# Broadcasting a norm's factor with eight narrow products instead of a diagonal, and another order of the second MLP pair's products

## The chip, the core and the metric

The kernel runs on one core of one Trainium2 chip. The core has a matrix engine (TensorE, PE in the profile; its weight loads are shown apart as PEld), a vector engine (VectorE, DVE), a scalar engine (ScalarE, ACT), a general engine (GpSimd, POOL) and a queue that issues DMA transfers (SyncE, SP). The metric is the device time of one execution in microseconds (us), lower is better.

## What is computed

One decoder layer over 1024 positions of width 1024, in float32. Cut to what matters here:

```python
h = rmsnorm(x, mix_norm)
q, k, v, su, sv, g_a, g_b = split(h @ w_in)
y_att = sliding_window_attention(q, k, v, q_norm, k_norm, sinks)
y_sgu = chunked_spatial_gating(su, sv, sgu_norm, w_s, b_s)
x = x + (sigmoid(g_a) * (y_att @ w_oa) + sigmoid(g_b) * (y_sgu @ w_ob)) @ w_out
z = rmsnorm(x, ffn_norm) @ w_up              # 1024 x 5632
z = conv_b + sum(conv_w[t] * shift(z, t) for t in range(3))   # causal, over positions
gate, val = split(z)                         # 2816 columns each
x = x + (silu(gate) * val) @ w_down
```

`rmsnorm(x, g)` is `x * rsqrt(mean(x * x) + 1e-6) * g`, with one factor per position.

## The kernel before, in words

The activations lie transposed: features on the 128 partitions, the 1024 positions along the row. A factor per position must therefore stand on every partition as a row of 1024 numbers, the tile `rstd_b`. It is first found as a column: position s * 128 + p on partition p, in column s of a 128 x 8 tile.

Every matrix product is made from numbers split into a high and a low part (`h` and `l`, type fp32r): high by high, high by low, low by high. ScalarE copies the high part (line 75), VectorE or GpSimd subtracts it to get the low one (line 974 for the weights of the MLP, on GpSimd).

**The broadcast.** `rms_rows` (line 120) turns the column into the row. VectorE makes a diagonal `diag` from the identity and the column (128 x 8 x 128); TensorE multiplies a matrix of ones with it, 512 columns at a time (line 123); ScalarE copies the result to `rstd_b` (line 125). These products are plain float32. It is done twice:
- In the prologue, for the first norm: the diagonal is made at line 322, the two halves are multiplied at lines 390 and 393, among the products of the queries (`q_proj`, lines 79 to 81) and the transposes of the keys (`k_trans`, line 338).
- In the MLP, for the second norm: `ssq_cols` (line 1338) multiplies the sums of squares with ones to get the column, VectorE and GpSimd turn it into the factor (GpSimd the power, line 116), and the diagonal is made at line 1349. Here the factor is a ratio: the activations were scaled before with the first norm's factor.

**The pairs.** The MLP's first half takes the 44 blocks of 128 columns of `w_up` in 22 pairs, a gate block and a value block. Each pair is computed with 7 products instead of 8, by sums and differences of the blocks (the scheme of Strassen and Winograd). A product is `prod(out, left, right)`: 12 matmuls, 4 steps of the contraction with three parts each, into one PSUM half of 512 columns. Left operands are weights: A11 and A12 (tile `p`, parts `ph` and `pl`), S1 and A22 (tile `q`, parts `qh` and `ql`), S3 (tile `s3`), S2 and S4 (the sums `lr` by GpSimd at line 608, parts in the tile AX). Right operands (B11, B21, B22, T1 to T4) are the activations, kept for all pairs. `more=True` adds onto what the output holds.

A pair has a gate accumulator (`g0`, `g1`) and a value accumulator (`v0`, `v1`). Copies of partial results in SBUF (`x1`, `x7`, `u2`) are added by VectorE in `sums` and `last_sum`; `scale` multiplies by `rstd_b`. Then come the convolution (`tap_v` and `tap_g` on ScalarE, line 1362, `conv` on VectorE, line 1367), `tanh` on ScalarE and `gated` on VectorE (lines 1390 and 1391), and the results go to memory. All that belongs to the previous pair runs while the current pair is multiplied.

**The order.** From the MLP on, and in the prologue's part around line 390, the order is written out by hand: every engine takes its instructions in the order of the program text. `first_pair` (line 1432) multiplies pair 0 and prepares pair 1: `nx.split_p`, `nx.split_s3`, `ssq_cols`, `nx.sums_r` (two `lr` on GpSimd), `nx.split_q` (`qh` on ScalarE, `ql` on GpSimd), `nx.split_r` (AX). Its results can't be scaled yet, as the factor isn't there. So the second pair (pair 1) is multiplied by `fast_pair` with `rms` given: the closure `rms` (line 1481) broadcasts the ratio into the PSUM tile of the second pair's own value accumulator, scales the first pair and adds its last sum. All later pairs call `fast_pair` with `rms=None`. The weight tiles are double buffered: `qh` and `ql` of a pair reuse the space that S1 and A22 of the pair before read; the tile of `s3h` is single.

The second pair's products before: A11, (broadcast), A12, S3, S1, A22, S2, S4.

Of the kernel before, what the change touches and what calls it, by code (L numbers as in the profile page):

```python
# [10 lines left out]
F = mybir.dt.float32  # L11
# [3 lines left out]
ALU = mybir.AluOpType  # L15
# [26 lines left out]
def body(ctx, tc, nc, a):  # L42
    L, H = slice(0, 512), slice(512, 1024)
# [6 lines left out]
    def nm(s):  # L50
        uid[0] += 1
        return f"{s}_{uid[0]}"
# [8 lines left out]
    def PS(s):  # L61
        pools_ = psum["P"]
        pools_.append(pools_.pop(0))
        return pools_[-1].tile([128, 1024], F, tag="P", name=nm(s))

    def PH(s):
        if psum.get("H") is None:
            return PS(s)[:, 0:512]
        return psum["H"].tile([128, 512], F, tag="H", name=nm(s))
# [32 lines left out]
    ident = base.tile([128, 128], F, name="ident")  # L102
    ones = base.tile([128, 128], F, name="ones")
    mh05 = base.tile([128, 16], F, name="mh05")
    rstd_b = base.tile([128, 1024], F, name="rstd_b")
    rstd = base.tile([128, 8], F, name="rstd")
# [6 lines left out]
    def rsqrt_cols(dst, ss, n, width):  # L113

        nc.vector.tensor_scalar(dst, ss, 1.0 / width, EPS, op0=ALU.mult, op1=ALU.add)
        return nc.gpsimd.tensor_tensor(dst, dst, mh05[:, :n], op=ALU.pow)

    msk = base.tile([128, 4, 128], U8, name="msk")

    def rms_rows(pb, diag, hs=(0, 1)):  # L120

        for h, p in zip(hs, pb):
            nc.tensor.matmul(p, ones, diag[:, h * 4:(h + 1) * 4, :], start=True, stop=True)
        for h, p in zip(hs, pb):
            nc.scalar.copy(rstd_b[:, h * 512:(h + 1) * 512], p)  # L125

# [48 lines left out]
    pa = pa_cm.__enter__()  # L175
# [30 lines left out]
    for k in range(8):  # L206
# [8 lines left out]
        for s in range(8):  # L215
            o = pkv[s // 4][:, (s % 4) * 256:(s % 4 + 1) * 256]
            c = slice(s * 128, (s + 1) * 128)
# [35 lines left out]
    def q_sq(n):  # L253
        p = st.pop(("pq", n)).rearrange("p (h d) -> p h d", d=64)
        sq = qp.tile([128, 4, 64], F, tag="qsq", name=nm("qsq"), bufs=2)
        nc.scalar.activation(sq, p, AF.Square)
        st[("q", n)] = [p, sq]
# [20 lines left out]
    def q_split(n):  # L278
        p = st.pop(("qT", n))
        qs = qp.tile([128, 2, 256], R, tag="qs", name=nm("qs"), bufs=2)  # L280
        for g in range(2):
            copy_hi(qs[ROWS[g], g, :], p[ROWS[g], :])
        for g in range(2):
            nc.vector.tensor_tensor(qs[ROWS[1 - g], g, :], p[ROWS[g], :], qs[ROWS[g], g, :].bitcast(F),
                                    op=ALU.subtract)
        st[("qT", n)] = qs
# [13 lines left out]
    for s in range(8):  # L300
        nc.tensor.matmul(p_ssq[:, 2 * s:2 * s + 2], sqsum[:, s * 128:(s + 1) * 128], ones[:, 0:2],
                         start=True, stop=True)
# [9 lines left out]
    for h in range(2):  # L312
# [5 lines left out]
    nc.vector.tensor_tensor(kss3, kss3, rstd2.unsqueeze(2).to_broadcast([128, 8, 2]), op=ALU.mult)  # L318
    rsqrt_cols(krs[:, 0:8], kss[:, 0:8], 8, 64)
    rsqrt_cols(krs[:, 8:16], kss[:, 8:16], 8, 64)  # L320
    diag = pa.tile([128, 8, 128], F, tag="sq", name="diag")
    nc.vector.tensor_tensor(diag, ident.unsqueeze(1).to_broadcast([128, 8, 128]),
                            rstd.unsqueeze(2).to_broadcast([128, 8, 128]), op=ALU.mult)
    q_sq(0)
    q_sq(1)

# [60 lines left out]
    q_split(0)  # L387
    q_trans(1)
    q_split(1)
    rms_rows([PH("rb")], diag, (0,))  # L390
    q_proj(3)
    k_trans(1)
    rms_rows([PH("rb")], diag, (1,))
    q_sq(2)
    v_split()
    q_ms(2)
# [320 lines left out]
    rb = sg.tile([128, 512], F, name="rb")  # L717
# [620 lines left out]
    def ssq_cols(p):  # L1338
        for s in range(8):
            nc.tensor.matmul(p[:, 2 * s:2 * s + 2], pools["sq2"][:, s * 128:(s + 1) * 128], ones[:, 0:2],  # L1340
                             start=True, stop=True)
        pool = pools["fp"]
        ss = pool.tile([128, 8], F, name="ss8b")
        nc.vector.tensor_copy(ss, p[:, 0:16].rearrange("p (s two) -> p s two", two=2)[:, :, 0])
        rsqrt_cols(ss, ss, 8, D)
        nc.vector.reciprocal(rstd, rstd)
        nc.vector.tensor_tensor(ss, ss, rstd, op=ALU.mult)
        diag = pool.tile([128, 8, 128], F, tag="ac", name="diag2", bufs=2)
        nc.vector.tensor_tensor(diag, ident.unsqueeze(1).to_broadcast([128, 8, 128]),
                                ss.unsqueeze(2).to_broadcast([128, 8, 128]), op=ALU.mult)  # L1350
        return diag

    class Pair(Blocks):

# [77 lines left out]
    def first_pair():  # L1432
        w, nx = lefts[0], lefts[1]
        z = PS("pz"), PS("pz")
        q, q2 = Pair(0, w.w, z[::-1]), Pair(1, nx.w)
        xu = pools["fp"].tile([128, 1024], F, tag="h", name="xu", bufs=2)
        x7, u2 = xu[:, L], xu[:, H]
        x1 = pools["fp"].tile([128, 512], F, tag="ac", name="x1", bufs=2)

        def late_split(n, r, eng):  # L1440
            comb[n] = Y(n, R, [128, 2, 4, 512])
            for k in range(0, 4, 2):
                src, h = pools[r][:, k:k + 2, :], comb[n][:, 0, k:k + 2, :]
                copy_hi(h, src)
                eng.tensor_tensor(comb[n][:, 1, k:k + 2, :], src, h.bitcast(F), op=ALU.subtract)

        q.prod(q.v1, "A11", "B11")
        nc.scalar.copy(x1, q.v1)
        w.split_r(0)
        nx.load_p()  # L1450
        q.prod(q.g0, "A12", "B21")
        late_split("T2", "raw2", nc.vector)
        nx.load_q()
        nx.load_s3()
        q.prod(q.g1, "S1", "T1")
        nc.scalar.copy(u2, q.g1)
        late_split("T4", "raw4", nc.gpsimd)
        for c, p in zip((L, H), late["px"]):
            nc.scalar.activation(p, late["ac"][:, c], AF.Square)
            nc.vector.tensor_tensor(pools["sq2"][:, c], pools["sq2"][:, c], p, op=ALU.add)  # L1460
        q.prod(q.v0, "S3", "T3")
        nc.scalar.copy(x7, q.v0)
        nx.split_p()
        nx.split_s3()
        nc.vector.tensor_tensor(x7, x7, u2, op=ALU.add)
        q.prod(q.g1, "S4", "B22", more=True)
        nc.vector.tensor_tensor(q.g0, q.g0, x1, op=ALU.add)
        q.prod(q.v1, "S2", "T2", more=True)
        pb = q2.zv
        diag = ssq_cols(pb)  # L1470
        nx.sums_r()
        nx.split_q()
        lefts[2].load_p()
        q.prod(q.v0, "A22", "T4", more=True)
        nc.scalar.copy(u2, q.v1)
        q.u2 = u2
        nx.split_r(1)
        nc.vector.tensor_tensor(q.v1, u2, x7, op=ALU.add)
        nc.vector.tensor_tensor(q.v0, u2, q.v0, op=ALU.add)

        def rms():

            rms_rows([pb[:, L], pb[:, H]], diag)
            q.scale(q.zv)
            q.last_sum()

        pools["ft_cm"] = tc.tile_pool(name="ft", bufs=1, reuse_waits="tile")
        return q, q2, rms

    def fast_pair(n, prev, q, hooks, rms=None):  # L1490

        nx = lefts[n + 1] if n + 1 < NPAIR else None

        def temp(t, p="ft"):
            return pools[p].tile([128, 512], F, tag=t, name=nm(t), bufs=2 if p == "ft" else 1)

        if rms:
            x1 = temp("x1f", "wx")
        else:
            prev.last_sum()  # L1500
            prev.tap_v()
            x1, x7, q.u2 = temp("x1"), temp("x7"), temp("u2")
        q.prod(q.g0, "A11", "B11")
        if nx:
            nx.load_q()
            nx.load_s3()
        else:
            hooks[2]()
        nc.scalar.copy(x1, q.g0)  # L1509
        if rms:  # L1510
            rms()
            pools["fp_cm"].__exit__(None, None, None)
            pools["ft"] = pools["ft_cm"].__enter__()
            x7, q.u2 = temp("x7"), temp("u2")
            prev.tap_v()
            q.prod(q.g0, "A12", "B21", more=True)
        prev.tap_g()
        prev.conv()
        q.prod(q.v0, "S3", "T3")
        if nx:  # L1520
            nx.split_s3()
        nc.scalar.copy(x7, q.v0)
        if not rms:
            q.prod(q.g0, "A12", "B21", more=True)
        if rms:
            nx.split_p()
        prev.tanh()
        if not rms:
            prev.gated()
        q.prod(q.g1, "S1", "T1")  # L1530
        if nx and not rms:
            nx.split_p()
        nc.vector.tensor_tensor(x7, x7, q.g1, op=ALU.add)
        if rms:
            prev.gated()
        prev.stores()
        if nx:
            nx.sums_r()
        if n + 2 < NPAIR:
            lefts[n + 2].load_p()  # L1540
        q.prod(q.v0, "A22", "T4", more=True)
        if nx:
            nx.split_q()
            nx.split_r(n + 1)
        else:
            hooks[0]()
        q.prod(q.v1, "S2", "T2")
        q.sums(x1, x7, q.v0)
        if not nx:
            hooks[1]()  # L1550
        q.prod(q.g1, "S4", "B22", more=True)
        return q

    SUM_AT = (2, 4, 5, 7, 8, 10)
# [280 lines left out]
```

## Time and profile before

| | us |
|---|---|
| median of 3 runs | 1198.6 |
| lowest and highest | 1198.53, 1199.31 |
| profiled execution, first to last instruction (span) | 1196.2 |
| TensorE busy in the span | 1183.4 (99%) |
| VectorE busy | 881.4 (74%) |
| ScalarE busy | 543.0 (45%) |
| GpSimd busy | 574.4 (48%) |
| matmuls of the MLP's pairs and the gates (line 1014), share of the chain that ended last | 42% |

For the profiled execution the span is all the time that is known; the median of the runs lies 2.4 us above it, which is what lies around the span.

A row of the timeline has the start and the duration in us, the engine, the line, the operation, output <- inputs, the shape, and how often it came in a row (xN); in brackets stands how long the engine was idle before it, and what ended that. A matmul shows a duration longer than the distance to the next one, since matmuls are pipelined: the pace is read from the starts. A row of waits has the engine and line that waited, what it waited for, the total in us, how often, and the longest. Names are those of tiles, with the buffer numbers left out.

### The profile page before, as it was taken

What the parts mean: (1) busy time and instruction counts of PE and PEld (TensorE: products, weight loads), DVE (VectorE), ACT (ScalarE), POOL (GpSimd) and SP (SyncE); (2) the same over time, 40 slices, a digit from 0 to 9 for tenths busy, and PEclk for the clock granted to TensorE, in tenths of its full rate; (3) what the DMA queues carried; (4) which work ended last, traced back from release to release, by engine and by line L of the source; (5) the groups of instructions that cost most, each with busy time, mean ns of one, the idle gap of its engine ahead of it and who ended that gap; (6) DMA issues with size and microseconds to landing.
All of it is one profiled execution on the core that took longest, in us unless ns stands there. A gap on an engine that the chain in (4) does not pass through costs nothing.

```text
span 1196.2 us, 15840 instructions
## 1 busy us (share of the span) xinstructions
PE 1183.4 (99%) x5866; PEld 1002.4 (84%) x5866; DVE 881.4 (74%) x1028; ACT 543.0 (45%) x832; POOL 574.4 (48%) x365
## 2 busy tenths in 40 slices
PE   9999999999999999999999999999999999999998
PEld 9889989988888888888788888888888888888886
DVE  8788975755638565668887788878788788775674
ACT  8555567644335222234444444444444445434331
POOL 2467685588668222344866575656657541000000
PEclk9999999999999999999999999999999999999999
DMA  7010143037786997342143342423333268975471
GB/s 283 23 53 19 54 139 126 11 122 271 237 308 206 358 320 273 128 166 98 45 150 108 104 136 102 149 89 123 109 129 124 87 205 290 370 235 194 150 238 61
DMA packets 79133, 191.27 MB, mean 160 GB/s; under 512 B 8912, under 2 KB 9168, under 8 KB 79056
## 3 DMA queue, kind: packets, MB, share of 16 engines
q1 hardware_dynamic: 79056, 190.26, 46.2%
q8 instruction: 46, 0.75, 0.3%
q14 instruction: 31, 0.25, 0.1%
HBM read 139.63 MB, written 50.59 MB: 159 GB/s over the span
## 4 chain that ended last, share of the span: by engine, by line
PE 82%; DVE 7%; ACT 4%; POOL 3%; DMA 2%; issue 2%; SPq 0%; ACTq 0%; POOLq 0%; DVEq 0%
PE pz L1014 42%; PE pd L1661 10%; PE pdy L1661 8%; PE po L80 2%; PE po L79 2%; PE po L81 2%; PE px L79 2%; PE px L80 2%; PE px L81 2%; DMA ls<-wup 1%; PE pvs L81 1%; PE pvs L79 1%; PE pvs L80 1%; ACT x L75 1%; PE pq L79 1%
## 5 line engine op out<-in xcount | busy, mean ns | idle before, releaser
L1014 PE MATMUL pz<-T,qh 128*128 128x512 f32 x472 | 145.6, 390 | 0.0
L1014 PE MATMUL pz<-B,ph 128*128 128x512 f32 x352 | 108.5, 389 | 0.7 <-ACT x1f L1509 0.7
L974 POOL TENSOR_TENSOR pl<-lp,ph 128x1024 fp32r<-128x1024 f32 x30 | 72.5, 2418 | 75.4 <-ACT ph L75 75.3
L1014 PEld LDWEIGHTS pz<-T,qh 128*128 128x128 f32 x472 | 88.4, 188 | 18.6 <-ACT u L865 0.3
L1014 PE MATMUL pz<-T,ql 128*128 128x512 f32 x236 | 91.8, 389 | 0.0
L96 POOL TENSOR_TENSOR wjl<-wj,wjh 128x512 fp32r<-128x512 f32 (+1 forms) x24 | 40.6, 1693 | 95.7 <-ACT wjh L75 95.7
L974 POOL TENSOR_TENSOR ql<-lq,qh 128x1024 fp32r<-128x1024 f32 x30 | 77.9, 2597 | 9.1 <-ACT qh L75 9.1
L1014 PEld LDWEIGHTS pz<-B,ph 128*128 128x128 f32 x352 | 66.0, 188 | 15.2 <-ACT x1f L1509 1.5
L1030 DVE TENSOR_TENSOR pz<-pz,rstd_b 128x1024 f32<-128x1024 f32 x60 | 73.9, 1232 | 3.3 <-ACT rstd_b L125 1.3
L974 POOL TENSOR_TENSOR s3l<-s,s3h 128x512 fp32r<-128x512 f32 x29 | 38.5, 1328 | 73.4 <-ACT s3h L75 73.4
L1014 PE MATMUL pz<-T,s3h 128*128 128x512 f32 x232 | 71.7, 390 | 0.0
L1014 PE MATMUL pz<-B,pl 128*128 128x512 f32 x176 | 68.5, 389 | 0.0
L1661 PE MATMUL pd<-bl,ah 128*128 128x512 f32 x176 | 68.5, 389 | 0.0
L1661 PE MATMUL pd<-bh,al 128*128 128x512 f32 x176 | 68.5, 389 | 0.0
L1661 PE MATMUL pd<-bh,ah 128*128 128x512 f32 x176 | 68.5, 389 | 0.0
L75 ACT ACTIVATE qh<-lq 128x1024 fp32r<-128x1024 f32 x30 | 31.8, 1061 | 72.0 <-POOL pl L974 36.6
L1014 PE MATMUL pz<-T,AX 128*128 128x512 f32 x264 | 63.4, 389 | 0.0
L1014 PE MATMUL pz<-B,AX 128*128 128x512 f32 x264 | 63.4, 389 | 0.0
L1014 PEld LDWEIGHTS pz<-T,AX 128*128 128x128 f32 x264 | 49.5, 188 | 10.3
L1014 PEld LDWEIGHTS pz<-B,AX 128*128 128x128 f32 x264 | 49.5, 188 | 10.3
L1367 DVE SCALAR_TENSOR_TENSOR tg<-pz,cp,tg 128x1023 f32<-128x1023 f32 (+1 forms) x44 | 56.2, 1278 | 0.8
L1367 DVE SCALAR_TENSOR_TENSOR tv<-pz,cp,tv 128x1023 f32<-128x1023 f32 (+1 forms) x44 | 56.2, 1277 | 0.8
(343 smaller groups left out, 3549.6 us busy)
## 6 DMA issues: line engine op xcount, KB each, us to landing
ls<-wup SPq DMA_DIRECT2D x22, 512.0 KB, 5.7
sum<-ls SPq DMA_DIRECT2D x22, 512.0 KB, 5.1
lp<-wup SPq DMA_DIRECT2D x22, 512.0 KB, 3.5
ra<-wdown SPq DMA_DIRECT2D x44, 256.0 KB, 4.8
b<-T SPq DMA_DIRECT2D x44, 256.0 KB, 3.8
B<-tv SPq DMA_DIRECT2D x33, 256.0 KB, 2.0
T<-tt SPq DMA_DIRECT2D x33, 256.0 KB, 2.1
b<-B SPq DMA_DIRECT2D x33, 256.0 KB, 3.5
```

The source lines that it names most:

```text
L75: return nc.scalar.activation(dst, src, AF.Copy, scale=scale)
L79: nc.tensor.matmul(out, wh, mh, start=first, stop=False, **kw)
L80: nc.tensor.matmul(out, wh, ml, start=False, stop=False, **kw)
L81: nc.tensor.matmul(out, wl, mh, start=False, stop=last, **kw)
L96: nc.gpsimd.tensor_tensor(l[:, :nk, :], r[:, :nk, :], h[:, :nk, :].bitcast(F), op=ALU.subtract)
L974: nc.gpsimd.tensor_tensor(l, r, h.bitcast(F), op=ALU.subtract)
L1014: nc.tensor.matmul(o, p[:, k, :], y[:, q, k, :], start=not more and k == 0 and j == 0, stop=k == 3 and j == 2, skip_group_check=True)
L1030: nc.vector.tensor_tensor(z, z, rstd_b, op=ALU.mult)
L1367: nc.vector.scalar_tensor_tensor(t[:, j:], p[:, 0:1024 - j], cw[:, ci, 2 - j:3 - j], t[:, j:], op0=ALU.mult, op1=ALU.add)
L1661: nc.tensor.matmul(o[d], p[:, k - k0, m], q[:, k - k0, :], start=new and k == 0 and j == 0, stop=k == HK - 1 and j == 2, skip_group_check= ...
```

## The change

The broadcast takes the column itself as weights: for each of the 8 columns, a product with 128 times the same column as stationary operand (a repeat with a step of zero) and the identity as moving operand gives 128 entries of the row, on all partitions. Four such products fill what one product of 512 columns filled before. Both diagonals are gone.

In the second pair, S1 goes ahead of the broadcast, S4 behind A12, and S2 ahead of A22. So the order is A11, S1, (broadcast), A12, S4, S3, S2, A22. The copy `x7` is taken from S1's result instead of S3's, and S3's result is added to it. The other pairs keep their order.

```diff
-    def rms_rows(pb, diag, hs=(0, 1)):
+    def rms_rows(pb, col, hs=(0, 1)):
         for h, p in zip(hs, pb):
-            nc.tensor.matmul(p, ones, diag[:, h * 4:(h + 1) * 4, :], start=True, stop=True)
+            for s in range(4):
+                c = 4 * h + s
+                nc.tensor.matmul(p[:, s * 128:(s + 1) * 128], col[:, c:c + 1].to_broadcast([128, 128]), ident,
+                                 start=True, stop=True)
...
-    diag = pa.tile([128, 8, 128], F, tag="sq", name="diag")
-    nc.vector.tensor_tensor(diag, ident.unsqueeze(1).to_broadcast([128, 8, 128]),
-                            rstd.unsqueeze(2).to_broadcast([128, 8, 128]), op=ALU.mult)
...
-    rms_rows([PH("rb")], diag, (0,))
+    rms_rows([PH("rb")], rstd, (0,))
...
-    rms_rows([PH("rb")], diag, (1,))
+    rms_rows([PH("rb")], rstd, (1,))
...
         nc.vector.tensor_tensor(ss, ss, rstd, op=ALU.mult)
-        diag = pool.tile([128, 8, 128], F, tag="ac", name="diag2", bufs=2)
-        nc.vector.tensor_tensor(diag, ident.unsqueeze(1).to_broadcast([128, 8, 128]),
-                                ss.unsqueeze(2).to_broadcast([128, 8, 128]), op=ALU.mult)
-        return diag
+        return ss
...
         nc.scalar.copy(x1, q.g0)
         if rms:
+            q.prod(q.g1, "S1", "T1")
             rms()
             pools["fp_cm"].__exit__(None, None, None)
             pools["ft"] = pools["ft_cm"].__enter__()
             x7, q.u2 = temp("x7"), temp("u2")
+            nc.scalar.copy(x7, q.g1)
             prev.tap_v()
             q.prod(q.g0, "A12", "B21", more=True)
+            q.prod(q.g1, "S4", "B22", more=True)
         prev.tap_g()
         prev.conv()
         q.prod(q.v0, "S3", "T3")
         if nx:
             nx.split_s3()
-        nc.scalar.copy(x7, q.v0)
+        if not rms:
+            nc.scalar.copy(x7, q.v0)
...
-        q.prod(q.g1, "S1", "T1")
+        if rms:
+            q.prod(q.v1, "S2", "T2")
+        else:
+            q.prod(q.g1, "S1", "T1")
         if nx and not rms:
             nx.split_p()
-        nc.vector.tensor_tensor(x7, x7, q.g1, op=ALU.add)
+        nc.vector.tensor_tensor(x7, x7, q.v0 if rms else q.g1, op=ALU.add)
...
-        q.prod(q.v1, "S2", "T2")
+        if not rms:
+            q.prod(q.v1, "S2", "T2")
         q.sums(x1, x7, q.v0)
         if not nx:
             hooks[1]()
-        q.prod(q.g1, "S4", "B22", more=True)
+        if not rms:
+            q.prod(q.g1, "S4", "B22", more=True)
         return q
```

More of the change, by code (lines that the diff above doesn't have):

```diff
@@ L1469, in first_pair @@
         pb = q2.zv
-        diag = ssq_cols(pb)
+        ratio = ssq_cols(pb)
         nx.sums_r()
@@ L1481, in rms @@
         def rms():
-            rms_rows([pb[:, L], pb[:, H]], diag)
+            rms_rows([pb[:, L], pb[:, H]], ratio)
             q.scale(q.zv)
```

## The prediction

> **What bounds the kernel now.** I read the page first, then the list of what TensorE waited for, then the timeline around the two places that the diff touches.
>
> ```profile
> PE 1183.4 (99%) x5866; PEld 1002.4 (84%) x5866; DVE 881.4 (74%) x1028; ACT 543.0 (45%) x832; POOL 574.4 (48%) x365
> ...
> PEclk9999999999999999999999999999999999999999
> ...
> PE pz L123 <- DVE diag L1349: 1.6, 1, 1.6
> ...
> PE pz L1014 <- ACT x1f L1509: 0.7, 1, 0.7
> ...
> PE pk L338 <- DVE kr L331: 0.6, 1, 0.6
> ```
>
> TensorE is busy for 99% of the span, so a change counts where it makes TensorE wait, stop waiting, or do other work. The diff touches three waits: 1.6 us for the diagonal of the MLP, 0.7 us right behind it, and 0.6 us in the prologue. About 2.9 us is all that it can remove. Everything else decides whether it adds waits. The stage of the first two, engine by engine:
>
> ```profile
> 567.41 2.88 PE L1014 MATMUL pz<-B,AX 128*128 128x512 f32 x12
> ...
> 579.93 0.39 PE L1014 MATMUL pz<-B,pl 128*128 128x512 f32 x1
> ...
> 581.90 1.98 PE L123 MATMUL pz<-diag,ones 128*128 128x512 f32 x4 [1.58 <-DVE diag L1349]
> ...
> 584.58 0.73 PE L1014 MATMUL pz<-B,ph 128*128 128x512 f32 x2 [0.70 <-ACT x1f L1509]
> ```
>
> A product is 12 matmuls: (2.88 - 0.39)/11 = 0.227 us from one to the next, 2.72 for the product. A11 of the second pair issues its last matmul at 579.93, so the next slot is 580.16. The broadcast starts at 581.90, and A12 only at 584.58. From slot to A12 the two waits and the broadcast take **4.42 us**.
>
> ```profile
> 577.65 1.65 POOL L116 TENSOR_TENSOR ss8b<-ss8b,mh 128x8 f32<-128x8 f32 x1
> 579.28 1.28 POOL L608 TENSOR_TENSOR lr<-lq,lp 128x512 f32<-128x512 f32 x1
> 580.64 2.33 POOL L608 TENSOR_TENSOR lr<-lp,lr 128x512 f32<-128x512 f32 x1
> 582.93 2.82 POOL L974 TENSOR_TENSOR ql<-lq,qh 128x1024 fp32r<-128x1024 f32 x1
> ...
> 577.46 1.06 ACT L75 ACTIVATE qh<-lq 128x1024 fp32r<-128x1024 f32 x1 [6.09 <-POOL pl L974]
> 583.00 1.06 ACT L75 ACTIVATE AX<-lr 128x1024 fp32r<-128x1024 f32 x1 [4.01 <-POOL lr L608]
> 583.96 0.57 ACT L1509 COPY x1f<-pz 128x512 f32<-128x512 f32 x1
> ...
> 579.34 1.25 DVE L1347 TENSOR_TENSOR ss8b<-ss8b,rstd 128x8 f32<-128x8 f32 x1 [2.75 <-POOL ss8b L116]
> 580.62 1.23 DVE L1349 TENSOR_TENSOR diag<-ident,ss8b 128x1024 f32<-128x1024 f32 x1
> 581.76 1.76 DVE L1478 TENSOR_TENSOR pz<-xu 128x512 f32<-128x512 f32 x1
> ```
>
> The GpSimd queue is full: the power for the norm, the two sums `lr` of S2 and S4, then `ql`, the low half of S1 and A22, which is ready only at 585.75. Now S1 is multiplied 5.4 us after A12 begins, and nobody notices. Each queue keeps program order: ScalarE's x1f copy has its data at 580.3, but stands behind the AX copy, which waits for `lr`.
>
> **The change part by part.** *The diagonal goes.* VectorE loses 1.23 us here; the column `ss8b` exists at 580.59. The rows also show VectorE and GpSimd excluding each other when both read two SBUF operands: an 8-column product took 1.25 us, ending as the first `lr` ends; the second `lr` took 2.33 us beside the diagonal where the first took 1.28. Without the diagonal, L1478 comes in its place, its own length about 0.69 (L1479, same shape, below), and `lr` ends at about 580.64 + 0.69 + 1.1 = 582.4 instead of 582.97. `ql` then runs with no rival, 2.4 us (a split without one takes 2.40, row 600.27 below), and ends at **584.8**: 0.9 us earlier.
>
> The Trainium skill (SBUF — State Buffer, section SBUF: two separate sides) says this of a pair of ports that VectorE, with two SBUF inputs, and GpSimd lock for a whole instruction. The 2.33 against 1.28 agree. By a reading that the engines only share bandwidth, `ql` would end some 0.3 us later.
>
> *S1 moves ahead of the broadcast.* Its first two matmuls use `qh` and go at 580.16; the third needs all of `ql`. TensorE stands from 580.61 to 584.87: **4.26 us of new wait**, with the broadcast, A12 and all later products queued behind it. So the wait for the diagonal is replaced by a longer one. The ten matmuls left end their slots at 587.14.
>
> *The broadcast.* Two products of 512 columns (four records) become eight of 128 columns (16 records), with a weight load each.
>
> ```profile
> 572.87 1.84 PE L1340 MATMUL pz<-ones,sq 128*128 128x2 f32 x16
> ...
> 1.05 3.36 PE L204 MATMUL warm<-ones 128*128 128x128 f32 x14 [1.05 <-POOL mh L108]
> ...
> 5.76 0.41 PE L79 MATMUL pkv<-wkv,x 128*128 128x256 f32 x1
> 5.97 0.41 PE L80 MATMUL pkv<-wkv,x 128*128 128x256 f32 x1
> ```
>
> Sixteen records with two columns each take (1.84 - 0.25)/15 = 0.106 us apiece: the load's floor. The only row of the very shape has 14 records in 3.36, (3.36 - 0.42)/13 = 0.226 apiece, but from the first microseconds, where a 256-column matmul took 0.21 us; at the products' later pace, 0.227 for 512 columns, it would be 0.114. Scaled by that, 0.226 becomes 0.12. I take 0.115, near the floor, so 1.85 us; the ends are 1.7 and 16 x 0.226 = 3.6. No row shows a column repeated by a zero step as weights. A12 then starts at 584.87 + 2.27 + 1.85 = 588.99. Before, S1 included, it would be 584.58 + 2.72 = 587.30: **+1.7 us**.
>
> *The products behind it.* The order is A12, S4, S3, S2, A22, five products, so the pair ends at 588.99 + 13.6 = **602.6** (601.0 before). Now A22 is last, and two things hang on the order:
>
> ```profile
> 590.30 0.64 ACT L75 ACTIVATE s3h<-s 128x512 fp32r<-128x512 f32 x1 [0.42 <-DMA s<-sum]
> ...
> 593.73 1.03 ACT L1387 ACTIVATE pz<-tg 128x1024 f32<-128x1024 f32 x1 [1.36 <-DVE tg L1367]
> 595.62 1.06 ACT L75 ACTIVATE qh<-lq 128x1024 fp32r<-128x1024 f32 x1 [0.85 <-PE pz L1014]
> 597.53 1.06 ACT L75 ACTIVATE AX<-lr 128x1024 fp32r<-128x1024 f32 x1 [0.85 <-POOL lr L608]
> 599.25 0.59 ACT L1024 COPY u<-pz 128x512 f32<-128x512 f32 x1 [0.65 <-DVE pz L1023]
> ...
> 602.59 1.21 ACT L1362 ACTIVATE tv<-pz,cp 128x1024 f32<-128x1024 f32 x1 [2.76 <-DVE pz L1030]
> 603.96 0.59 ACT L1509 COPY x<-pz 128x512 f32<-128x512 f32 x1 [0.16 <-PE pz L1014]
> ...
> 583.56 0.69 DVE L1479 TENSOR_TENSOR pz<-xu,pz 128x512 f32<-128x512 f32 x1
> ...
> 596.06 1.22 DVE L1391 TENSOR_TENSOR tv<-pz,tv 128x1024 f32<-128x1024 f32 x1
> ...
> 600.27 2.40 POOL L974 TENSOR_TENSOR AX<-lr,AX 128x1024 fp32r<-128x1024 f32 x1
> ```
>
> The next pair's `s3h` reuses the tile that S3 reads (590.30 is just after S3's end); S3's last slot now ends at 597.15, so `s3h` goes at 597.4, `ph` at 598.0, on GpSimd the 2.4 us of `pl` end at 601.8 and the two `lr` at 604.8 (1.28 each, and 0.3 for a subtraction of VectorE that comes between, an estimate from L1478's case). The next `qh` waits for A22 to free its buffer (before at 595.62, A22's end): now 602.8. ScalarE then does AX at 604.85, and only behind it the copy `u`, 605.9 (before: 599.25). From `u` to the tap of the next pair is the same chain of VectorE as before, 602.59 - 599.25 = 3.3 us, so the tap goes at 609.2 and the copy of A11 right behind it, 1.21 + 0.57, ends at 611.0 (before: 604.55). The third pair's A12 accumulates onto that copy's source. TensorE reaches it at 602.6 + 2 x 2.72 = 608.05 and waits **3.0 us**. Before, the copy had about 1.9 us to spare (606.45 - 604.55).
>
> Nothing else is late: S4 needs the copy x7 (about 590.3) at 591.7, and A11 of the third pair overwrites what `gated` reads (L1391, ended at 597.28): tanh now stands behind `ph`, 599.0 instead of 593.73, so that read ends about 602.5, only just in time for 602.6. Of DMAs the diff moves none; on SP the next `lq` loads wait for `ql`, late by 7 us but needed a whole pair later.
>
> *What follows.* This ring (sums, tap, conv, tanh, `ph`, `lr`, AX, `u`) runs by itself, slower than TensorE:
>
> ```profile
> 614.66 1.06 ACT L75 ACTIVATE qh<-lq 128x1024 fp32r<-128x1024 f32 x1 [3.13 <-POOL pl L974]
> 617.45 1.06 ACT L75 ACTIVATE AX<-lr 128x1024 fp32r<-128x1024 f32 x1 [1.73 <-POOL lr L608]
> ...
> 957.38 1.07 ACT L75 ACTIVATE qh<-lq 128x1024 fp32r<-128x1024 f32 x1 [2.31 <-issue]
> 960.98 1.06 ACT L75 ACTIVATE AX<-lr 128x1024 fp32r<-128x1024 f32 x1 [2.54 <-POOL lr L608]
> ```
>
> Over these 18 pairs AX moves 343.53 us and `qh`, which marks A22's end, 342.72: the ring loses 0.8 us, out of the spare 1.9 us, so today it costs nothing. With the spare gone, TensorE goes at the ring's pace: 0.3 us at the fourth pair, then 0.09 per two pairs, together **+1.1 us**. Below is none of it (0), above 1.9.
>
> *Prologue.* The same lock:
>
> ```profile
> 35.50 1.22 DVE L322 TENSOR_TENSOR diag<-ident,rstd 128x1024 f32<-128x1024 f32 x1
> ...
> L116 POOL TENSOR_TENSOR krs<-krs,mh x2: 1632/2125/2618, 35.6 to 38.2; 128x8 f32<-128x8 f32 x2
> ...
> 38.25 0.17 DVE L329 TENSOR_TENSOR krs<-krs,rstd 128x8 f32<-128x8 f32 x1 [0.93 <-POOL krs L116]
> ```
>
> The first power beside the diagonal took 2.62 us, the second 1.63. Free of it, `krs` comes 1 us earlier, and the 0.6 us wait at L338 falls away. VectorE's queue behind it moves up by about 0.54, and q_proj(3), bound by VectorE's `qs`, with it; the first half's broadcast hides under that wait, the second costs 0.1. I take **-0.45 us**, between -0.75 and 0.4 (the 0.226 price).
>
> *Sum:* +1.7 + 3.0 + 1.1 - 0.45 = **+5.3 us** on the profiled execution: its span is 1196.2, so 1201.5. The times shown have a median of 1198.6, 2.4 above that span for what lies around it; the same 2.4 gives **1203.9 us**.
>
> **Rivals.**
> 1. *Only the first wait comes* (ScalarE's `u`, or the `lr` before AX, is earlier than walked): +1.7 - 0.45 = 1199.9 us. For it: the walk is seven steps long, and one 2 us off would do. Against: each step has a row, and 3 us is much.
> 2. *The queues follow readiness and not the program.* Then GpSimd does `ql` as soon as `qh` is there (578.52): 578.6 to 581.0, before the power. S1 stalls 0.45 us, the broadcast starts at 583.3, A12 at 585.2: 2.1 us earlier than 587.30, and `u` is not held up behind AX. With the prologue -2.6: 1196.0, faster. It decides if `ql` ends before about 581.1. Against: x1f stood 3.7 us in line with its data there.
> 3. *The weight load of a repeated column is slow*, 0.226 a record: +1.8 here and +0.8 in the prologue: 1206.5.
> 4. *The clock falls in the 4.3 us gap.* No wait of TensorE here is as long (the longest is the 1.6 us), and the clock row of the page is all nines; but the first microseconds show matmuls at half pace, 0.21 instead of 0.114. Were it so again for as long as those (about 4 us), half of 4 is lost: 1205.9. The Trainium skill (TensorE: Matmul & The Clock Gate, Part 1) says that an idle window of about 3.4 us halves the clock, the window running freely; no run here shows it in mid-kernel.
>
> That the change doesn't do what it says is no case of its own: 2 and 3 are its forms.
>
> **How the numbers follow.** Forecast 0.68 (its own range 1202.5 to 1205.2); rival 1 0.11; rival 2 0.05; rival 3 0.04; rival 4 0.12. The range from 1200.8 to 1206.4 leaves out rivals 1, 2 and most of 3, under 0.2. About 0.2% (2.4 us) is what a measurement of this kernel can tell from no change: faster takes rival 2 (0.05), same takes rival 1 and a little of the forecast's edge (0.12), slower has the rest (0.83).
>
> **What would show it.** A wait of TensorE for `ql` (POOL L974) near 4.3 us in S1; none for the column; A12 of the third pair waiting about 3 us for ScalarE's copy; small waits of the same kind at later pairs; L338 no longer waiting. I am wrong if S1 doesn't stall, if `u` comes before 604, or if the 16 records take over 2.5 us.

## The result, and the profile after

The changed kernel takes **1206.37 us** (median of 5 runs, 1205.84 to 1207.31); the kernel before, beside it, 1199.14 us (1198.53 to 1199.85). The ratio is 1.0063, with a 95% interval from 1.0051 to 1.0075: slower by 7.2 us, where 5.3 were predicted. The profiled spans are 1204.7 and 1196.2 us. They differ by 8.5 us, more than the medians: in every run of the changed kernel the time is 1.7 us above its span, and by that the profiled execution before was one of 1197.9 us, about 1.2 below its median.

The page's first lines, busy time and clock:

```profile
PE 1186.3 (98%) x5890; PEld 1003.6 (83%) x5890; DVE 879.8 (73%) x1026; ACT 541.5 (45%) x832; POOL 572.4 (48%) x365
...
PEclk9999999999999999999899999999999999999999
```

TensorE is busy 3 us longer with the same products (24 more records are those of the broadcasts), and one slice of the clock row has fallen to 8: matmuls there ran slower. What TensorE waited for (engine and line, the awaited thing, us in total, times, longest):

```profile
PE pz L1014 <- ACT x1f L1506: 3.6, 1, 3.6
PE pz L1014 <- ACT x L1513: 1.7, 1, 1.7
PE pz L1014 <- ACT x L1506: 1.4, 1, 1.4
...
PE pz L1014 <- DVE x L1537: 0.8, 1, 0.8
```

The waits for the diagonal and for `kr` are gone. Four new ones stand in their place, 7.5 us, and only the third (the third pair's A12) is named in the prediction as it came. TensorE's timeline around them:

```profile
579.02 0.39 PE L1014 MATMUL pz<-B,pl 128*128 128x512 f32 x1
583.05 1.22 PE L1014 MATMUL pz<-T,qh 128*128 128x512 f32 x2 [3.64 <-ACT x1f L1506]
584.07 0.63 PE L1014 MATMUL pz<-T,ql 128*128 128x512 f32 x1
...
587.91 0.53 PE L1014 MATMUL pz<-T,ql 128*128 128x512 f32 x1
588.28 1.95 PE L125 MATMUL pz<-ident,ss8b 128*128 128x128 f32 x16
591.88 0.72 PE L1014 MATMUL pz<-B,ph 128*128 128x512 f32 x2 [1.65 <-ACT x L1513]
...
603.85 0.73 PE L1014 MATMUL pz<-T,qh 128*128 128x512 f32 x2 [0.78 <-DVE x L1537]
...
613.70 0.73 PE L1014 MATMUL pz<-B,ph 128*128 128x512 f32 x2 [1.39 <-ACT x L1506]
```

A11's last matmul starts at 579.02, so the next slot is 579.25. S1 starts at 583.05, and its third matmul, the first with `ql`, at 584.07, where it would have stood at 579.70 without a wait: 4.37 us (the first two took 1.02 us instead of 0.45, already at half pace, so a little of that is the clock's). The ten matmuls from there take 588.28 - 584.07 = 4.21 us instead of 2.27: half pace. Then the broadcast, and A12 at 591.88. GpSimd, ScalarE and VectorE beside that, one after the other:

```profile
581.39 2.35 POOL L974 TENSOR_TENSOR ql<-lq,qh 128x1024 fp32r<-128x1024 f32 x1
...
581.47 1.06 ACT L75 ACTIVATE AX<-lr 128x1024 fp32r<-128x1024 f32 x1 [3.39 <-POOL lr L608]
582.43 0.57 ACT L1506 COPY x1f<-pz 128x512 f32<-128x512 f32 x1
590.26 1.07 ACT L128 COPY rstd_b<-pz 128x512 f32<-128x512 f32 x2 [7.26 <-PE pz L125]
591.22 0.60 ACT L1513 COPY x<-pz 128x512 f32<-128x512 f32 x1
...
603.11 0.69 DVE L1537 TENSOR_TENSOR x<-x,pz 128x512 f32<-128x512 f32 x1 [3.64 <-PE pz L1014]
```

The thing to see is which tile each wait concerns. S1 writes `g1`; `x1f` is a copy of `g0`. S1 doesn't use what is copied, but `g0` and `g1` are halves of one accumulator tile. The waits fit one reading, which experiments 4 to 6 test by moving the copies: in the compiled program the wait goes by the whole tile. So S1 starts only when the copy ends (583.00), and that copy stands in ScalarE's queue behind AX. Likewise A12, on `g0`, waits for the copy `x7` of `g1`, which stands behind the two copies of the broadcast (1.65 us). And VectorE's sum onto `x7`, which reads S3's result in `v0`, waits for the end of S2 in `v1`, while A22 on `v0` waits for that sum (0.78).

The same stage in windows (length, busy us of PE, PEld, DVE, ACT and POOL, then the granted clock, share of DMA, GB/s):

```profile
580.00:585.00 5.00, 1.95 (x5) 1.51 (x6) 1.02 (x2) 1.53 (x2) 5.00 (x3) 0.64 0.38 111
585.00:590.00 5.00, 5.00 (x25) 4.29 (x23) 0.00 (x0) 0.00 (x0) 1.08 (x1) 0.68 0.49 151
```

The granted clock is 0.64 and 0.68 (1.00 in the windows on both sides): (0.36 + 0.32) x 5 = 3.4 us of clock are missing, which is 6.8 us at half rate. The rows at half pace, S1's, lie within. The Trainium skill (TensorE: Matmul & The Clock Gate, Part 1) says that an idle window of about 3.4 us halves the clock until a busy one has passed, and that the windows run freely. The length agrees, as 6.8 us are two of them. If an idle window means one without any matmul, the moment of the fall does not. Here is the clock's fall in the changed kernel, and below it S1's start and the fall in experiment 8, whose gap ahead of S1 is equally long:

```profile
581.00:581.50 0.50, 0.00 (x0) 0.00 (x0) 0.05 (x1) 0.03 (x1) 0.50 (x2) 0.87 0.00 0
581.50:582.00 0.50, 0.00 (x0) 0.00 (x0) 0.00 (x0) 0.50 (x1) 0.50 (x1) 0.50 0.00 0
```
```profile
582.60 0.73 PE L1014 MATMUL pz<-T,qh 128*128 128x512 f32 x2 [3.64 <-ACT x1f L1506]
...
584.00:584.50 0.50, 0.50 (x3) 0.38 (x2) 0.00 (x0) 0.00 (x0) 0.50 (x1) 0.56 0.30 86
```

A mean of 0.87 over half a microsecond means that the last 0.13 us of it ran at half rate. So the changed kernel's clock fell at about 581.4, only 2.0 us after A11's last matmul ended (579.41). In experiment 8 it fell at about 584.1, when S1 had already run for 1.5 us. How idle a window must be, no run here settles.

Where the time went, against the profile before, counted from the slot behind A11 (which lies 0.9 us earlier than before; in the other profiles with this prologue it lies between 578.5 and 580.2, so most of the 0.9 may be chance):

| | predicted | measured |
|---|---|---|
| stall ahead of S1's third matmul | 4.26 | 4.37 |
| S1 at half pace | 0 (a rival) | 1.94 |
| the broadcast, 16 records at 0.112 | 1.85 | 1.79 |
| A12 behind `x7` | 0 | 1.81 |
| less the 4.42 us of before | -4.42 | -4.42 |
| **A12 begins later by** | **1.7** | **5.5** |
| five products to the pair's end (A22's wait in them) | 0 | 1.1 |
| third pair's A12 | 3.0 | 1.7 |
| the ring, fourth pair to the last | 1.1 | 1.0 |
| up to the slot behind A11 | -0.45 | -0.9 |
| **sum** | **5.3** | **8.4** |

The span is later by 8.5 us. So the table explains this pair of executions; which rows hold the 1.2 us by which the profiled execution before was a short one is not known.

### The profile page after: what moved, and what is told of

Same layout as the page of the kernel before. It is cut to its first block, busy times and chain, and to the rows that moved or that the text cites. A ratio compares the mean times of both kernels' runs of the same rounds, so it can differ in the third digit from the quotient of the medians.

```text
span 1204.7 us, 15883 instructions
## 1 busy us (share of the span) xinstructions
PE 1186.3 (98%) x5890; PEld 1003.6 (83%) x5890; DVE 879.8 (73%) x1026; ACT 541.5 (45%) x832; POOL 572.4 (48%) x365
## 4 chain that ended last, share of the span: by engine, by line
PE 88%; DVE 4%; ACT 3%; POOL 3%; issue 1%; DMA 1%; SPq 0%; POOLq 0%; ACTq 0%; DVEq 0%
PE pz L1014 46%; PE pd L1667 10%; PE pdy L1667 7%; PE px L81 2%; PE px L80 2%; PE po L81 2%; PE po L80 2%; PE po L79 2%; PE px L79 2%; PE pvs L79 1%; PE pvs L81 1%; PE pvs L80 1%; PE pq L79 1%; PE pq L81 1%; PE pq L80 1%
## 5 line engine op out<-in xcount | busy, mean ns | idle before, releaser
L974 POOL TENSOR_TENSOR AX<-lr,AX 128x1024 fp32r<-128x1024 f32 x22 | 53.2, 2420 | 3.5 <-ACT AX L75 3.5
```

Of the source, the lines that this page charges most:

```text
L974: nc.gpsimd.tensor_tensor(l, r, h.bitcast(F), op=ALU.subtract)
```

## The experiments

Each diff is against the changed kernel, unless said otherwise; only what matters of it is shown. Times are medians; the kernel before, run beside them, had 1198.7 us (1198.4 in experiments 10 and 12). The changed kernel was not run again beside them: a difference to it is one to the 1206.37 us above, whose ratio has the interval from 1.0051 to 1.0075. The intervals of experiments 2 to 5 and 8 overlap that one, so there the rows of the profile carry the argument, and the difference of the times is only a hint.

**1 and 2: each half of the change by itself.** First the new broadcast in both places, with the order of before:

```diff
-            q.prod(q.g1, "S1", "T1")
             rms()
...
-            nc.scalar.copy(x7, q.g1)
...
-            q.prod(q.g1, "S4", "B22", more=True)
...
+        nc.scalar.copy(x7, q.v0)
+        q.prod(q.g1, "S1", "T1")
...
+        q.prod(q.v1, "S2", "T2")
...
+        q.prod(q.g1, "S4", "B22", more=True)
```

> The new broadcast in both places, with the old order of the second pair's products. If the order is what costs, this is faster than before by about 1 us, near 1198.1: the column is there 1.25 us before the diagonal was, but A12 still waits for ScalarE's copy behind AX, which comes only about 0.55 earlier, and the prologue gives about 0.45. If the eight narrow products themselves cost, it is at or above 1199.6.

Measured 1196.96 us, ratio 0.9983 (0.9975 to 0.9991). Its TensorE rows:

```profile
579.31 2.05 PE L125 MATMUL pz<-ident,ss8b 128*128 128x128 f32 x16 [0.36 <-DVE ss8b L1347]
...
582.59 0.72 PE L1014 MATMUL pz<-B,ph 128*128 128x512 f32 x2 [1.23 <-ACT x1f L1506]
```

The column costs a wait of 0.36 us where the diagonal cost 1.58; A12 then waits 1.23 us for `x1f` instead of 0.70, as that copy still stands behind AX. Now the other half, the new order with both diagonals kept (`rms_rows` and `ssq_cols` as before):

```diff
-                nc.tensor.matmul(p[:, s * 128:(s + 1) * 128], col[:, c:c + 1].to_broadcast([128, 128]), ident,
-                                 start=True, stop=True)
+            nc.tensor.matmul(p, ones, diag[:, h * 4:(h + 1) * 4, :], start=True, stop=True)
```

> Both diagonals kept, only the new order of the second pair's products. If the order is what costs, this is at least as slow as the whole change, 1206 to 1208 (the diagonal makes the sums on GpSimd, and so ql and the copy x1f, about 0.6 us later). If the broadcast costs, it is near 1199.

Measured 1208.34 us, ratio 1.0078 (1.0064 to 1.0093). So the order costs 9.6 us and the broadcast gives 1.7; together 7.9, beside 7.2 measured for the whole change.

**3: a cover for the gap.** One more product A11 into `v1` ahead of S1 (`SPARE` is 1). Its result is overwritten by the broadcast; the rest of the kernel is the same.

```diff
         if rms:
+            for _ in range(SPARE):
+                q.prod(q.v1, "A11", "B11")
             q.prod(q.g1, "S1", "T1")
```

> The whole change, with one product done once more than needed (A11 by B11 into a place that the broadcast overwrites) in the gap ahead of S1: 2.7 of the about 4.4 us of idle time are filled. If the idle time makes the clock fall, the granted clock stays 1.00, S1's last ten matmuls take 2.3 us instead of 4.2, and the time is about 1205.5 or a little below, with no run of mean clock 0.996. If the fall has another cause, nothing changes: 1206 to 1207.

Measured 1204.96 us, ratio 1.0047 (1.0034 to 1.006): 1.4 us less than the changed kernel, with 2.7 us more work. Its timeline (lines are one higher) and the same two windows:

```profile
583.92 0.73 PE L1015 MATMUL pz<-T,qh 128*128 128x512 f32 x2 [0.92 <-ACT x1f L1507]
584.69 0.51 PE L1015 MATMUL pz<-T,ql 128*128 128x512 f32 x1
...
587.10 1.95 PE L126 MATMUL pz<-ident,ss8b 128*128 128x128 f32 x16
```
```profile
580.00:585.00 5.00, 4.05 (x17) 2.75 (x16) 1.86 (x3) 1.53 (x2) 4.92 (x4) 1.00 0.31 83
585.00:590.00 5.00, 4.04 (x26) 3.44 (x24) 0.00 (x0) 0.92 (x2) 1.98 (x1) 1.00 0.56 179
```

The clock stays at 1.00, and S1's ten matmuls take 587.10 - 584.69 = 2.41 us, not 4.21. So the gap costs its own length and, through the clock, about 1.9 us more in the profile; the times show 1.4.

**4: the copy `x7` ahead of the broadcast's copies** on ScalarE (for the pools' sake the column lies in another pool, and the sum of `last_sum` onto `g1` is made in `first_pair`):

```diff
             q.prod(q.g1, "S1", "T1")
-            rms()
             pools["fp_cm"].__exit__(None, None, None)
             pools["ft"] = pools["ft_cm"].__enter__()
             x7, q.u2 = temp("x7"), temp("u2")
             nc.scalar.copy(x7, q.g1)
+            rms()
```

> The whole change, with ScalarE's copy x7 of S1's result ahead of the broadcast's two copies (for it the pool of the temporaries opens earlier, the first pair's last sum is added ahead of the broadcast, and the column stands in another pool). If A12 waits for the copy of the other half of its accumulator, its wait of 1.65 us goes, and the time falls by 1.5 to 2 us, to about 1204.5. If A12 waited for the broadcast's row, nothing changes: 1206 to 1207.

Measured 1204.39 us, ratio 1.0046 (1.0033 to 1.006), 2.0 us less than the changed kernel. All the rows of TensorE between A11 and the third pair's A12 that show a wait:

```profile
584.03 1.22 PE L1014 MATMUL pz<-T,qh 128*128 128x512 f32 x2 [3.63 <-ACT x1f L1507]
...
602.11 0.73 PE L1014 MATMUL pz<-T,qh 128*128 128x512 f32 x2 [0.78 <-DVE x L1538]
...
611.95 0.73 PE L1014 MATMUL pz<-B,ph 128*128 128x512 f32 x2 [1.39 <-ACT x L1507]
```

A12's wait is gone and the other three stand as they were, so the wait of 1.65 us is a matter of ScalarE's queue and not of S1's data. Not all of the 2.0 us is this wait, however: the clock fell for half as long in this profile (its windows stand in the last section).

**5 and 6: `ql` or `x1f`?** In the changed kernel `x1f` ends at 583.00, just before S1's first matmul, and `ql` at 583.74, just before the third; its trace doesn't show what either alone is worth. First `ql` ahead of the sums on GpSimd; then that, and the copy `x1f` ahead of the AX split:

```diff
+        nx.split_q()
         nx.sums_r()
-        nx.split_q()
...
-        nx.split_r(1)
...
         nc.scalar.copy(x1, q.g0)
         if rms:
+            lefts[1].split_r(1)
```

> The whole change, with the split of q (qh, ql) ahead of the two sums lr on GpSimd; ql is ready at about 580.9. If S1 waits for ql alone, as the prediction had it, S1 starts 3 us earlier, and the time is about 1202 to 1203. If S1's first matmul waits for ScalarE's copy x1f of the other half of its accumulator, which stands behind AX and so behind lr, S1 starts later than before, at about 585.5 to 586, and the time is 1207.5 to 1209.

> As the run with ql first, and the copy x1f ahead of the AX split on ScalarE. Then nothing holds S1 but ql: it stalls about 1.2 us instead of 4.4, the clock stays at 1.00, and A12 still waits for x7. About 1201.7. If something else holds S1, the time stays above 1205.

With `ql` early: 1208.92 us, ratio 1.0081 (1.0067 to 1.0095): no faster, by the medians even slower. Its GpSimd, ScalarE and TensorE rows:

```profile
577.63 2.35 POOL L974 TENSOR_TENSOR ql<-lq,qh 128x1024 fp32r<-128x1024 f32 x1
...
583.10 1.06 ACT L75 ACTIVATE AX<-lr 128x1024 fp32r<-128x1024 f32 x1 [5.79 <-POOL lr L608]
584.07 0.57 ACT L1506 COPY x1f<-pz 128x512 f32<-128x512 f32 x1
...
584.68 1.22 PE L1014 MATMUL pz<-T,qh 128*128 128x512 f32 x2 [6.04 <-ACT x1f L1506]
```

`ql` is there at 579.98, and S1 still waits, for `x1f`, whose place behind AX has become worse. With both mended: 1201.92 us, ratio 1.0024 (1.0013 to 1.0034), 4.5 us less than the changed kernel:

```profile
580.73 0.73 PE L1014 MATMUL pz<-T,qh 128*128 128x512 f32 x2 [0.68 <-ACT x1f L1505]
...
587.44 0.74 PE L1014 MATMUL pz<-B,ph 128*128 128x512 f32 x2 [1.65 <-ACT x L1513]
```

S1 waits 0.68 us, about the copy's own length (0.58), and the clock stays up (1.00 in the windows from 580 to 590). So S1 needs both, and the prediction knew of one. The copy early with `ql` late was not run; `ql` is an input of S1.

**7: the broadcast alone, with `x1f` ahead of AX** (experiment 1 and, from the last diff, this move):

```diff
-        nx.split_r(1)
...
+            lefts[1].split_r(1)
```

> The new broadcast with the old order, and the copy x1f ahead of the AX split on ScalarE. The broadcast goes right when the column is there, and A12 right behind it: TensorE's waits of 1.6 and 0.7 us fall to about 0.4 in all. With the prologue about 2.5 us faster than before, near 1196.6. If the ring of ScalarE, GpSimd and VectorE then takes over, the gain is under 1.5 us.

Measured 1196.68 us, ratio 0.9979 (0.9971 to 0.9988). A12 follows the broadcast with no wait in its profile, but the time can't be told from the 1196.96 of experiment 1: inconclusive, where about 0.4 us was at stake. The wait has also moved on, to A22, which in experiment 1 had none:

```profile
591.27 0.73 PE L1014 MATMUL pz<-T,qh 128*128 128x512 f32 x2 [0.79 <-ACT x L1519]
```

**8: A22 ahead of S2** (order A12, S3, S4, A22, S2):

```diff
-            q.prod(q.g1, "S4", "B22", more=True)
...
         if rms:
-            q.prod(q.v1, "S2", "T2")
+            q.prod(q.g1, "S4", "B22", more=True)
...
+        q.prod(q.v1, "S2", "T2")
         q.sums(x1, x7, q.v0)
```

> The whole change, with the products behind the broadcast in the order A12, S3, S4, A22, S2: VectorE's sum into x7 needs only S3, and A22 frees its weights one product earlier. If S2 ahead of A22 is what makes the late waits, the 0.8 us at A22 and most of the 1.4 us at the third pair's A12 go, and the drift behind them: about 1203. If they come from the late broadcast alone, 1205.5 or more.

Measured 1203.66 us, ratio 1.0041 (1.0029 to 1.0054), 2.7 us less than the changed kernel. The third pair's wait:

```profile
610.79 0.73 PE L1014 MATMUL pz<-B,ph 128*128 128x512 f32 x2 [0.41 <-ACT x L1506]
```

It falls from 1.39 to 0.41 us, and A22 waits no more for the sum onto `x7`. These two waits are 1.8 of the 2.7 us. About 0.6 more is the clock's, which fell for half as long: S1 and the broadcast begin at 582.60 and 587.21, 4.61 us apart instead of 5.23.

**9: all four places mended at once** (the diffs of 4, 6 and 8 together, the core of which is):

```diff
+            lefts[1].split_r(1)
             q.prod(q.g1, "S1", "T1")
-            rms()
...
             nc.scalar.copy(x7, q.g1)
+            rms()
...
-            q.prod(q.v1, "S2", "T2")
+            q.prod(q.g1, "S4", "B22", more=True)
```

> The changed kernel with every wait taken away that the other runs named: ql ahead of the sums, the copy x1f ahead of the AX split, the copy x7 ahead of the broadcast's copies, A22 ahead of S2. Theory (the new order costs only through those four places): from the kernel with ql and x1f first (1201.9), less the 1.65 us wait of A12 for x7, less the 2.7 us that A22 ahead of S2 gave back: about 1197.5 us, no wait over 0.7 us of TensorE in this stage, clock 1.00. Rival (something unnamed in the order costs time, or the ring stays out of step): above 1200.

Measured 1200.14 us, ratio 1.0011 (1.0003 to 1.002): faster than the changed kernel by 6.2 us, but 2.6 above what was expected. The rival was partly right. Its TensorE rows and the first of VectorE's sums:

```profile
595.12 0.73 PE L1014 MATMUL pz<-T,qh 128*128 128x512 f32 x2 [0.75 <-DVE x L1537]
...
606.71 0.73 PE L1014 MATMUL pz<-B,ph 128*128 128x512 f32 x2 [0.41 <-ACT x L1506]
...
600.90 0.70 DVE L1023 TENSOR_TENSOR pz<-x1f,pz 128x512 f32<-128x512 f32 x1 [1.86 <-PE pz L1014]
```

A22's wait is back, as it is now reached earlier. And the sum at L1023, the ring's start, needs S2, which this order puts last: it waits 1.86 us, where before it waited 0.47. Experiment 8 had mended one wait of the ring (for A22) and made another. The expectation had also counted all of the 2.7 us of experiment 8, with the clock's 0.6 in it, which the kernel of experiment 6 no longer loses.

**10: the same, with S2 ahead of A22 and S4 last** (diff against experiment 9):

```diff
         if rms:
-            q.prod(q.g1, "S4", "B22", more=True)
+            q.prod(q.v1, "S2", "T2")
...
-        q.prod(q.v1, "S2", "T2")
+        if not rms:
+            q.prod(q.v1, "S2", "T2")
         q.sums(x1, x7, q.v0)
...
+        q.prod(q.g1, "S4", "B22", more=True)
```

> The kernel with all four places mended, but S2 ahead of A22 and S4 last. In the run before it (S4 ahead of A22, S2 last: 1200.14 us) VectorE's first sum waits 1.86 us for the end of S2, the last product, so the tap of the next pair still comes late: the third pair's A12 waits 0.41 us (0.77 by the distance of the qh rows, 17.09 instead of 16.32) and the ring then loses 0.32 us and 0.66 more. Theory (the rest of the cost is the ring: the sums must not hang on the last product): with S2 early the tap comes some 1.6 us earlier, the third pair waits no more, and most of the 0.98 us goes: 1200.14 - 0.77 - 0.8 = about 1198.5. Rival (the rest sits in the second pair itself): no change, 1200.1.

Measured 1197.80 us, ratio 0.9995 (0.9986 to 1.0004). VectorE's and ScalarE's rows:

```profile
599.49 0.68 DVE L1023 TENSOR_TENSOR pz<-x1f,pz 128x512 f32<-128x512 f32 x1
...
603.75 1.21 ACT L1359 ACTIVATE tv<-pz,cp 128x1024 f32<-128x1024 f32 x1 [2.76 <-DVE pz L1030]
...
614.87 1.07 ACT L75 ACTIVATE qh<-lq 128x1024 fp32r<-128x1024 f32 x1 [2.19 <-issue]
...
957.65 1.06 ACT L75 ACTIVATE qh<-lq 128x1024 fp32r<-128x1024 f32 x1 [1.35 <-issue]
```

The sum no longer waits, the third pair's wait is gone, and from the third pair to the last, A22 ends every 19.04 us on average, as before: 957.65 - 614.87 = 342.78, where before it was 342.72. The ring holds nobody up. The time can't be told from that of the kernel before; what is left of the order's cost, beside the broadcast alone, experiment 12 measures.

**11: the new broadcast in the prologue alone** (against the kernel before; `rms_rows_col` is the changed kernel's `rms_rows`):

```diff
-    diag = pa.tile([128, 8, 128], F, tag="sq", name="diag")
...
-    rms_rows([PH("rb")], diag, (0,))
+    rms_rows_col([PH("rb")], rstd, (0,))
...
-    rms_rows([PH("rb")], diag, (1,))
+    rms_rows_col([PH("rb")], rstd, (1,))
```

> The kernel before with the new broadcast in the prologue alone (the MLP keeps its diagonal and its order). The prediction gave this part -0.45 us, the trace of the changed kernel speaks for -0.7: 1198.0 to 1198.3 against 1198.7, no wait at the place where kr was waited for (0.6 us before), the two powers krs about 1.63 us each. Rival (the rest of the prologue hides or eats it): 0, 1198.7. And if the part in the prologue is about -0.6, the broadcast in the MLP brings the other -1.1 of the -1.7 us that the new broadcast alone measured.

Measured 1197.18 us, ratio 0.9988 (0.9979 to 0.9997): -1.5 us, with an interval from -2.5 to -0.4. It is faster, but the size is too rough for the split that was expected, and what the broadcast alone gives in the MLP (1196.96 less this) can't be told from nothing. GpSimd's row:

```profile
35.73 3.24 POOL L116 TENSOR_TENSOR krs<-krs,mh 128x8 f32<-128x8 f32 x2 [0.70 <-DVE krs L115]
```

Both powers together take 3.24 us, where before they took 2.62 and 1.63: the one that lay beside the diagonal is as short as the other now. The wait for `kr` is gone.

**12: the kernel of experiment 1 again, beside that of 10** (same diff as there):

> The new broadcast alone (both places) in the old order once more, on the chip of the run above, so that the two stand beside each other. Theory (S1 ahead of the broadcast has nothing left to cover once the diagonal is gone, and gives the ring a later start): this one is faster than the mended order by 1 to 2 us, about 1197.0. Rival (S1 as cover for the column is worth something): the mended order is as fast, or faster.

Measured 1197.34 us, ratio 0.9988 (0.9978 to 0.9997), beside 1197.80 for the mended order. The 0.5 us between them lie within both intervals, so the expected 1 to 2 us did not come: once these waits are mended, S1 ahead of the broadcast neither costs nor gives anything that can be measured. The broadcast alone is faster than the kernel before, by 1.0 us here and 1.7 in experiment 1, and than the changed one.

## Why the prediction was right or wrong

- **The time.** 1206.37 us is above the forecast's own range (1202.5 to 1205.2) and only just inside the outer one, which ends at 1206.4. Two terms were put at nothing, the waits behind the copy `x7` and the clock, 4.8 us together, and the third pair's wait was put 1.3 us too high. That the total came out so near is partly luck. The 2.4 us added for what lies around the span were 1.7 in each run; the other 0.7 went in because the profiled execution before was a short one.
- **Direction right, mechanism right in part.** The new order puts S1 where its inputs are not ready, then makes the third pair wait and sets the ring's pace; the broadcast and the prologue give a little back. Experiments 1 and 2 show the two signs. Rivals 1 and 2 fell: `u` came at 608.64, not earlier than the 605.9 of the walk, and `x1f` again stood in line behind AX.
- **The stall ahead of S1: right in size (4.37 for 4.26 us), half right in cause.** The step said that two matmuls go at once and the third waits for `ql`. In fact the first already waited, for `x1f`. Two queues, GpSimd's and ScalarE's, happened to end within a microsecond of each other (583.74 and 583.00), so that the size came out right is luck. Experiment 5 shows that mending the predicted cause alone gains nothing.
- **"Nothing else is late: S4 needs the copy x7 at 591.7": the step that failed.** The copy was late for A12, not for S4, since both halves of the accumulator wait as one: 1.81 us, and the wait is gone in experiment 4. The same goes for A22 behind the sum onto `x7`: 1.1 us with the slots around it. Behind A11 the sum lacked 3.5 us (5.3 + 0.45 predicted, 9.3 measured): 1.8 and 1.1 of this step, 1.9 of the clock, less 1.3 that the third pair's wait was overrated.
- **The clock: a rival at 0.12 that should have been in the sum.** A gap of over 4 us was the forecast itself, and it halved the clock, for 1.94 us in the profile. The rival's price, 2 us, was right; its total, 1205.9, was near the measured time only because the two other errors, 2.9 and -1.3, partly cancel. By experiment 3 its cover gives 1.4 us on the median. In three of five runs of the changed kernel the mean clock was 0.996, in two 0.999; their means are 1206.9 and 1205.9 us, so how long it falls seems to vary.
- **The third pair's wait: right in cause, mis-sized** (1.7 for 3.0 us). The ring was as late as walked, and a little more (the tap at 611.97 instead of 609.2), but TensorE came 4.1 us later than walked (pair's end 606.71 instead of 602.6). A second stall behind a first one shrinks by what the first one already delayed:

```profile
606.73 1.06 ACT L75 ACTIVATE qh<-lq 128x1024 fp32r<-128x1024 f32 x1 [4.03 <-POOL lr L608]
...
608.64 0.56 ACT L1024 COPY u<-pz 128x512 f32<-128x512 f32 x1
611.97 1.20 ACT L1359 ACTIVATE tv<-pz,cp 128x1024 f32<-128x1024 f32 x1 [2.76 <-DVE pz L1030]
...
622.01 1.06 ACT L75 ACTIVATE qh<-lq 128x1024 fp32r<-128x1024 f32 x1 [1.11 <-issue]
...
965.75 1.06 ACT L75 ACTIVATE qh<-lq 128x1024 fp32r<-128x1024 f32 x1 [1.35 <-issue]
```

- **The ring's drift: right.** From 622.01 to 965.75 are 343.74 us instead of 342.72: 1.0 for the 1.1 predicted, in steps too short for the list of waits. The eight profiles in which the third pair waits all begin it with 0.3 us at the fourth pair. Experiment 10, with the spare time back, has none of it. But the profile of experiment 12, where the third pair doesn't wait, has 343.39, so 0.7 us of drift can also come in an execution without that wait.
- **The broadcast: right** (0.112 us a record for 0.115). Rival 3 fell.
- **The prologue: right in sign** (experiment 11), its size open: -0.4 to -2.5 us there, -0.45 predicted. Of the 0.9 us up to A11, 0.5 is a wait at line 1100 that stands only in the profile before and that the diff doesn't touch.

## What to carry to other kernels

Before an instruction is moved, look for everything that holds its output tile, the other half of an accumulator included, and for the place of each of those in its own queue: here the waits went by the tile, not by the elements. If a forecast contains a gap of TensorE of 4 us, it should hold two prices: here they were the gap itself and the half-rate time after it. And a chain with less than 2 us to spare should be walked again for each new order, as a mended wait often only hands the chain to the next product in line.

## What the runs showed of the hardware

- The clock fell to half in mid-kernel in all five profiles with a gap of 3.6 to 6.0 us ahead of S1 (the changed kernel, experiments 2, 4, 5 and 8). It did not after gaps of 0.92 us (experiment 3), 1.58 (the kernel before) and 1.65 (experiment 6). In some profiles the fall was half as long: the windows of experiment 4,

```profile
580.00:585.00 5.00, 1.37 (x4) 0.72 (x3) 2.60 (x4) 1.53 (x2) 4.92 (x4) 0.90 0.25 81
585.00:590.00 5.00, 5.00 (x25) 4.33 (x25) 0.00 (x0) 0.58 (x1) 2.05 (x1) 0.76 0.52 181
```

  miss (0.10 + 0.24) x 5 = 1.7 us of clock, 3.4 us at half rate, against 6.8 in the changed kernel.
- A column repeated by a zero step is hardly slower as weights than the matrix of ones at line 1340: 16 records of 128 columns in 1.95 us, (1.95 - 0.275)/15 = 0.112 apiece (0.275 is the length of one), about the 0.106 of two columns, so at this width the moving data cost next to nothing.
